# One-hot delivery of the last expert's rows to the first gate tile, and gate weights split earlier, in a hybrid transformer block

## The chip, the cores and the metric

The kernel runs on one core of one Trainium2 chip. The metric is the device time of one execution, in microseconds (us). Three runs of the kernel before took 1682.45, 1684.27 and 1686.49 us, with a median of 1684.27 us. The profile shown here is of one more execution, whose own time was 1682.92 us.

## The reference

One layer over 1024 tokens of width 1024, in float32:

```python
h = rms_norm(x, norm_mix);  z = h @ w_in
x = x + concat(pool_mix(z), neighbourhood_attention(z)) @ w_out
x = x + expert_choice_ffn(rms_norm(x, norm_ffn), w_router, w_gate, w_up, w_down)
g = sigmoid(rms_norm(x, norm_ple) @ w_ple_gate)
e = rms_norm(p @ w_ple_proj, norm_ple_post)
x = x + g * e
```

The expert part has 16 experts. Each picks its 128 best tokens (top-k over the tokens), so that a token can be picked by several experts or by none. For its tokens an expert computes `silu(xe @ w_gate) * (xe @ w_up) @ w_down` with 2048 hidden columns, scales the row by the token's affinity, and adds it to the token's row of the result. The change concerns the seam between this part and the last one, the gate: a product of all 1024 rows with a 1024 x 1024 matrix.

## The kernel before

**Staging.** The residual rows live in DRAM, as `acc_rows` (1024 x 1024). Each expert gathers its 128 rows by an indirect DMA on POOL's queue, computes, and adds its result `ye` to `acc_rows` by an indirect DMA with accumulation, also on POOL's queue (line 994: the scatter). After the last expert the gate reads `acc_rows` back in eight tiles of 128 tokens (`x2_0` to `x2_7`, line 1035; all of them are called x in the rows).

**Products.** Every float32 product is made of three passes over two-part numbers: an operand is split into `hi`, its rounded copy, and `lo`, what is left; `mm3` adds hi x hi (line 94), lo x hi (line 96) and hi x lo (line 98). A split takes one ACT instruction (line 85, or 88 with a gain) and one DVE instruction (line 86, or 89 with a gain). The left operand is split when its rows are transposed (`turn_rows`, line 931: four transposes of 128 x 128 on the tensor engine PE, then one split of 128 x 512).

**Weights.** Weights stream in as chunks of 256 x 1024 (1 MB) on the DMA queue of SP: 24 chunks for an expert and 4 for the gate, 388 in all, numbered through. `feed` splits half a chunk (128 x 1024) into a pair of buffers `fhi`, `flo`, of which there are four pairs (NH = 4). `product` uses the oldest split half and then calls `feed`, so that splitting runs four halves ahead of PE: each new ACT instruction waits until PE has left the buffer. Twelve raw slots go round in `ring`; when both halves of a chunk are split its slot is free and the next chunk is loaded into it, up to `NFREE = len(chunks) - 2`. With `feed(keep=True)` the split half goes to a raw slot instead of a buffer pair and stays there (called `fhl`).

**Order.** On PE, and in the expert stage on DVE and ACT too, instructions stand in the order of the program; after the expert stage (`steady.close()`) a scheduler sets the order on DVE and ACT. Each expert runs `expand` four times over (gate half 0, up half 0, gate half 1, up half 1: four steps of two products) and then `contract` (the down product into `pd`: eight steps kk of two products). During expert 14, `match` and `index` make expert 15's one-hot matrix `oh` of 128 x 1024, its token numbers `ix`, and start its gather.

**The seam.** During the last `contract`, the products' own `feed` calls split the last halves of the down weights and the first four halves of the gate weights. Then ACT scales `pd` into `ye` (line 993), the scatter is issued, and a gate chunk is loaded behind it on POOL's queue; SP loads `x2_0`, the last gate chunk, `x2_1` and `x2_2`. The rows of `x2_0` are transposed and split, the other four gate halves are split with `feed(True)`, and the eight embedding tiles `es` (128 x 1024 each) are multiplied by `g_post` on DVE (line 1082).

**The gate.** A gate block takes one tile of 128 tokens: 16 groups of three matmuls of 512 columns (two output halves j, eight steps k), with the transposes of the next tile put in front of groups 6 and 9. `sg` is the sigmoid of an output half (ACT, line 1062), multiplied by `es` and added to `x2` (DVE, lines 1063 and 1064) and stored.

## Time and profile before

| | us |
|---|---|
| median of three runs | 1684.27 |
| the profiled execution | 1682.92 |
| its span, first to last instruction | 1681.2 |
| PE busy | 1630.8 (97%) |
| DVE busy | 1347.5 (80%) |
| ACT busy | 1153.9 (69%) |
| POOL busy | 169.1 (10%) |

Section 2 of the page cuts the span into 40 slices; PE's busy share in tenths and the granted clock of PE read

```profile
PE   8999998998899999999999999999999999999698
PEclk9999999999999999999999999999999999999799
```

A slice is 42 us. PE is busy throughout the expert stage (slices 12 to 37), dips in slice 38, where the clock dips too, and is busy again to the end. Matmuls overlap their neighbours: a pass of 512 columns lasts 0.39 us in the rows, but the next one starts 0.227 us after it. So the start of an instruction is the better mark. "x2" behind a group means two instructions merged into a row, and the value in square brackets is the idle time of the engine ahead of them, with what ended it.

### The profile page before, as it was taken

The page shows a single profiled execution, that of the slowest core. Times are in us where ns is not written, and L with a number is a line of the kernel's source. Part 1 is how long each engine was busy: PE and PEld are TensorE (multiplying, and loading weights), DVE is VectorE, ACT ScalarE, POOL GpSimd, SP SyncE. Part 2 cuts the span into 40 slices and gives each one's busy share as a digit, 9 for nine tenths or more (in the row PEclk, how much of TensorE's full clock was granted, in tenths as well). Part 3 has the DMA queues.
Part 4 walks back from the last instruction along what each step waited for, and adds up shares of the span by engine and source line. Part 5 has one row for each costly group of instructions (what it writes and reads, how often), then busy time and mean ns, then how long its engine had stood idle before and what let it go on. Part 6 is the DMA issues. An engine that isn't in the chain of part 4 may idle for free.

```text
span 1681.2 us, 22945 instructions
## 1 busy us (share of the span) xinstructions
PE 1630.8 (97%) x8165; PEld 1368.0 (81%) x8165; DVE 1347.5 (80%) x1866; ACT 1153.9 (69%) x1471; POOL 169.1 (10%) x216
## 2 busy tenths in 40 slices
PE   8999998998899999999999999999999999999698
PEld 6889998886778888888888888888888888888587
DVE  4474555459879999999999999999999999999632
ACT  6254554432488888888888888888888888888431
POOL 1111112243310000000000000000000000000100
PEclk9999999999999999999999999999999999999799
DMA  6301201363699999999999999999999999996321
GB/s 187 116 29 33 66 26 51 92 204 97 216 365 373 401 371 400 377 368 408 373 391 385 367 403 377 378 399 369 399 378 367 410 370 392 386 368 242 106 98 59
DMA packets 129266, 470.54 MB, mean 280 GB/s; under 512 B 9600, under 2 KB 14720, under 8 KB 129152
## 3 DMA queue, kind: packets, MB, share of 16 engines
q1 hardware_dynamic: 122848, 445.80, 70.3%
q0 software_dynamic: 6304, 23.28, 5.3%
q8 instruction: 64, 1.05, 0.3%
q14 instruction: 50, 0.41, 0.1%
HBM read 448.00 MB, written 21.04 MB: 279 GB/s over the span
## 4 chain that ended last, share of the span: by engine, by line
PE 84%; DVE 7%; issue 4%; DMA 2%; POOL 1%; ACT 1%; SPq 0%; DVEq 0%; ACTq 0%; POOLq 0%
PE pu L94 7%; PE pu L96 7%; PE pu L98 7%; PE pg L94 6%; PE pg L96 6%; PE pd L96 6%; PE pd L94 6%; PE pg L98 6%; PE pd L98 6%; DVE both L581 3%; PE proj L94 2%; PE proj L98 2%; PE proj L96 2%; PE py L375 2%; PE pq L94 2%
## 5 line engine op out<-in xcount | busy, mean ns | idle before, releaser
L86 DVE TENSOR_TENSOR flo<-fraw,fhi 128x1024 fp32r<-128x1024 f32 x768 | 916.3, 1222 | 71.0 <-ACT fhi L85 33.5
L85 ACT ACTIVATE fhi<-fraw 128x1024 fp32r<-128x1024 f32 x768 | 809.4, 1061 | 192.6 <-PE pd L96 72.6
L94 PE MATMUL pd<-fhi,hidT 128*128 128x512 f32 x512 | 162.1, 398 | 0.0
L94 PE MATMUL pg<-fhi,xeT 128*128 128x512 f32 x512 | 159.2, 392 | 0.7 <-ACT xeT L85 0.7
L94 PE MATMUL pu<-fhi,xeT 128*128 128x512 f32 x512 | 159.2, 392 | 0.0
L96 PE MATMUL pd<-fhi,hidT 128*128 128x512 f32 x512 | 158.4, 390 | 0.0
L98 PE MATMUL pd<-flo,hidT 128*128 128x512 f32 x512 | 158.0, 390 | 0.0
L96 PE MATMUL pu<-fhi,xeT 128*128 128x512 f32 x512 | 158.0, 390 | 0.0
L96 PE MATMUL pg<-fhi,xeT 128*128 128x512 f32 x512 | 157.9, 389 | 0.0
L98 PE MATMUL pg<-flo,xeT 128*128 128x512 f32 x512 | 157.8, 389 | 0.0
L98 PE MATMUL pu<-flo,xeT 128*128 128x512 f32 x512 | 157.6, 389 | 0.0
L98 PEld LDWEIGHTS pd<-flo,hidT 128*128 128x128 f32 x512 | 96.1, 188 | 20.7
L96 PEld LDWEIGHTS pd<-fhi,hidT 128*128 128x128 f32 x512 | 96.1, 188 | 20.6
L96 PEld LDWEIGHTS pg<-fhi,xeT 128*128 128x128 f32 x512 | 96.0, 188 | 20.4 <-DVE xeT L86 0.4
L98 PEld LDWEIGHTS pu<-flo,xeT 128*128 128x128 f32 x512 | 96.1, 188 | 20.3
L96 PEld LDWEIGHTS pu<-fhi,xeT 128*128 128x128 f32 x512 | 96.1, 188 | 20.3
L98 PEld LDWEIGHTS pg<-flo,xeT 128*128 128x128 f32 x512 | 96.1, 188 | 20.1
L94 PEld LDWEIGHTS pg<-fhi,xeT 128*128 128x128 f32 x512 | 94.9, 188 | 19.7 <-ACT xeT L85 1.0
L94 PEld LDWEIGHTS pu<-fhi,xeT 128*128 128x128 f32 x512 | 95.0, 188 | 18.8
L94 PEld LDWEIGHTS pd<-fhi,hidT 128*128 128x128 f32 x512 | 92.8, 188 | 16.6
L994 POOL DMA_INDIRECT acc_rows<-ye,ix x16 | 26.6, 1661 | 764.0 <-ACT ye L993 764.0
L94 PE MATMUL proj<-wph,xT 128*128 128x384 f32 x256 | 99.8, 390 | 0.0
(215 smaller groups left out, 2341.0 us busy)
## 6 DMA issues: line engine op xcount, KB each, us to landing
fraw<-in_w_gate_dram SPq DMA_DIRECT2D x128, 1024.0 KB, 7.2
fraw<-in_w_down_dram SPq DMA_DIRECT2D x128, 1024.0 KB, 9.2
fraw<-in_w_up_dram SPq DMA_DIRECT2D x127, 1024.0 KB, 7.7
x<-in_x_dram SPq DMA_DIRECT2D x15, 512.0 KB, 4.9
wp_raw<-in_w_qkv_dram SPq DMA_DIRECT2D x16, 384.0 KB, 4.6
h_rows<-x POOLq DMA_DIRECT2D x8, 520.5 KB, 4.0
wo_raw<-in_w_out_dram SPq DMA_DIRECT2D x8, 512.0 KB, 3.4
acc_rows<-x SPq DMA_DIRECT2D x8, 512.0 KB, 4.6
```

The costliest lines, as they stand in the source:

```text
L85: ACT.activation(hi, src, AF.Copy)
L86: DVE.tensor_tensor(lo, src, hi.bitcast(F32), op=ALU.subtract)
L94: PE.matmul(outs[j], xh, wh[j], start=start, stop=False)
L96: PE.matmul(outs[j], xl, wh[j], start=False, stop=False)
L98: PE.matmul(outs[j], xh, wl[j], start=False, stop=stop)
L375: PE.matmul(pys[t][:, h], PTs[t, h][:, j * P:(j + 1) * P], vs[NU * pr + u0 + j][:, h * HD:(h + 1) * HD], start=(j == 0), stop=(j == u1 - u ...
L581: DVE.tensor_tensor(b[:, :, j], a[:, :, 0], a[:, :, 1], op=(ALU.max, ALU.min)[j])
L994: return POOL.indirect_dma_start(out=acc, out_offset=bass.IndirectOffsetOnAxis(ap=idxs[e][:, :1], axis=0), in_=ye, in_offset=None, compute ...
```

## The change

The rows of the last expert go two ways. They are still added to `acc_rows` by the scatter. In addition, `x2_0` is loaded during the last expert (behind step kk = 2 of its first up product), and the part of the last expert's result that belongs to tokens 0 to 127 is added to it on the core: `here` is a one-hot matrix (128 x 128, float32: row r has a one in the column of its token if that is below 128), and two float32 products `px = here^T ye` of 512 columns are added to `x2_0` by DVE. `ye` is made in two halves. Twelve transposes of the identity stand around the two products on PE.

The last `contract` splits more: `feed(True)` is called twice behind each of the steps 3, 4 and 5, the number of halves ahead grows to 6 and 8 and then falls to 0, so that the steps 6 and 7 feed nothing. All four gate chunks are loaded in the normal stream. The last two gate halves are split after the rows of `x2_0`. The `es` products may not be issued ahead of the split of those rows, and in gate block 0 the transposes of tile 1 stand in front of groups 13 and 15 in place of 6 and 9.

```diff
-    NFREE = len(chunks) - 2
+    NFREE = len(chunks)
...
+        if e == E - 1:
+            ixf = ixt[:, 1:2].bitcast(F32)
+            DVE.tensor_reduce(ixf, pi[:, 0:2], axis=AX.X, op=ALU.add)
+            here = fw.tile([P, D // 2], F32, tag="oh", name="here")
+            DVE.tensor_scalar(here[:, :P], iota, ixf, None, op0=ALU.is_equal)
+            ohs["first"] = here[:, :P]
...
     def product(po, xh, xl, start, stop):
         hi, lo = fed.pop(0)
         mm3([po[:, 0], po[:, 1]], xh, xl, halves(hi), halves(lo), start, stop)
-        if len(fed) < NH:
+        if len(fed) < ahead[0]:
             feed()
+
+    ahead = [NH]
...
-        ACT.activation(ye, pd.rearrange("p a b -> p (a b)"), AF.Copy, scale=xes[e][:, D + e:D + e + 1])
+        af = xes[e][:, D + e:D + e + 1]
+        if e < E - 1:
+            ACT.activation(ye, pd.rearrange("p a b -> p (a b)"), AF.Copy, scale=af)
+        else:
+            px = [fps.tile([P, 2, 512], F32, tag=t, name=f"px_{t}", bufs=1)[:, 0] for t in ("pg", "pu")]
+            wps = fps.tile([P, 4, P], F32, tag="tr", name="warm_ps3")
+            for i in range(8):
+                PE.transpose(wps[:, i % 4, :], ident, ident)
+            for h in range(2):
+                hs = slice(h * 512, (h + 1) * 512)
+                ACT.activation(ye[:, hs], pd[:, h], AF.Copy, scale=af)
+                PE.matmul(px[h], ohs["first"], ye[:, hs], start=True, stop=True)
+                DVE.tensor_tensor(x2s[0][:, hs], px[h], x2s[0][:, hs], op=ALU.add)
+            for i in range(4):
+                PE.transpose(wps[:, i, :], ident, ident)
         return POOL.indirect_dma_start(out=acc, out_offset=bass.IndirectOffsetOnAxis(ap=idxs[e][:, :1], axis=0),
                                 in_=ye, in_offset=None, compute_op=ALU.add)
...
+            if e == E - 1 and kk == 2:
+                load_x2(0)
...
+            if e == E - 1 and 3 <= kk < 6:
+                feed(True)
+                feed(True)
+                ahead[0] = (NH + 2, NH + 4, 0)[kk - 3]
...
-    with tc.issue_after(done.ins):
-        load_chunk(eng=POOL)
-    got = load_x2(0)
-    with tc.issue_after(got.ins):
-        load_chunk()
     for i in range(1, 3):
         load_x2(i)
     turn2(0, 0)
-    turn2(0, 1)
+    last = turn2(0, 1)
+    feed()
+    feed()
     norm2(0)
-    for _ in range(4):
-        feed(True)
-    for t in es:
-        for b in range(2):
-            DVE.tensor_tensor(t[:, b], t[:, b], gp, op=ALU.mult)
+    steady.close()
+    with tc.issue_after(last.ins):
+        for t in es:
+            for b in range(2):
+                DVE.tensor_tensor(t[:, b], t[:, b], gp, op=ALU.mult)
     for i in range(NU):
         sides = {}
         if i + 1 < NU:
-            sides[6] = [lambda i=i: turn2(i + 1, 0)]
-            sides[9] = [lambda i=i: turn2(i + 1, 1), lambda i=i: norm2(i + 1)]
+            sides[6 if i else 13] = [lambda i=i: turn2(i + 1, 0)]
+            sides[9 if i else 15] = [lambda i=i: turn2(i + 1, 1), lambda i=i: norm2(i + 1)]
```

On DVE, from the last down weights to the first output of the gate, the order before is this (fraw with its number is a raw chunk, hgT the split transposed rows of a gate tile):

```order
L89 SCALAR_TENSOR_TENSOR flo_0_14515<-fraw_14264,vec,fhi_0_14514 128x1024
L89 SCALAR_TENSOR_TENSOR flo_1_14525<-fraw_14264,vec,fhi_1_14524 128x1024
L1082 TENSOR_TENSOR es_4572<-es_4572,g_post 128x1024 x2
L1082 TENSOR_TENSOR es_4573<-es_4573,g_post 128x1024 x2
L1082 TENSOR_TENSOR es_4574<-es_4574,g_post 128x1024 x2
L1082 TENSOR_TENSOR es_4575<-es_4575,g_post 128x1024
L89 SCALAR_TENSOR_TENSOR fhl_0_14569<-fraw_14538,vec,fhl_0_14569 128x1024
L86 TENSOR_TENSOR hgT_14548<-tr_g_0_14549,hgT_14548 128x512
L86 TENSOR_TENSOR hgT_14548<-tr_g_1_14556,hgT_14548 128x512
```

and this in the changed kernel, from the last gate halves that are split ahead of `ye`:

```order
L88 SCALAR_TENSOR_TENSOR fhl_0_14509<-fraw_14294,vec,fhl_0_14509 128x1024
L88 SCALAR_TENSOR_TENSOR fhl_1_14512<-fraw_14294,vec,fhl_1_14512 128x1024
L1019 TENSOR_TENSOR x_0_14142<-px_pg,x_0_14142 128x512
L1019 TENSOR_TENSOR x_0_14142<-px_pu,x_0_14142 128x512
L86 TENSOR_TENSOR hgT_14572<-tr_g_0_14573,hgT_14572 128x512
L86 TENSOR_TENSOR hgT_14572<-tr_g_1_14580,hgT_14572 128x512
L1105 TENSOR_TENSOR es_4572<-es_4572,g_post 128x1024
L88 SCALAR_TENSOR_TENSOR flo_0_14588<-fraw_14316,vec,fhi_0_14587 128x1024
L88 SCALAR_TENSOR_TENSOR flo_1_14592<-fraw_14316,vec,fhi_1_14591 128x1024
```

The split of tile 0's rows has moved ahead of all `es` products, and two halves of gate weights stand behind the first of them. The next instructions of DVE there are

```order
L1105 TENSOR_TENSOR es_4572<-es_4572,g_post 128x1024
L1105 TENSOR_TENSOR es_4573<-es_4573,g_post 128x1024 x2
L1105 TENSOR_TENSOR es_4574<-es_4574,g_post 128x1024 x2
L1105 TENSOR_TENSOR es_4575<-es_4575,g_post 128x1024 x2
L1089 TENSOR_TENSOR sg_0_14636<-sg_0_14636,es_4572 128x512
L86 TENSOR_TENSOR hgT_14656<-tr_g_0_14657,hgT_14656 128x512
L1090 TENSOR_TENSOR sg_0_14636<-sg_0_14636,x_0_14142 128x512
L86 TENSOR_TENSOR hgT_14656<-tr_g_1_14670,hgT_14656 128x512
```

The split of tile 1's rows (hgT_14656) stands behind all eight `es` products and behind the first `sg` product; before, no `es` product stood between the two tiles' splits but one. On ACT, where the sums of squares (junkg) of tiles 1 and 2 stand ahead of the first sigmoid in both kernels, the changed order is

```order
L1017 ACTIVATE ye_14539<-pd_14359,xe_13553 128x512 x2
L1060 ACT_TABLE_LOAD
L1060 ACTIVATE warm_14562<-warm 128x1
L85 ACTIVATE hgT_14572<-tr_g_0_14573 128x512
L85 ACTIVATE hgT_14572<-tr_g_1_14580 128x512
L87 ACTIVATE fhi_0_14587<-fraw_14316,vec 128x1024
L87 ACTIVATE fhi_1_14591<-fraw_14316,vec 128x1024
L1066 ACTIVATE junkg_14596,ssqg_14595<-x_0_14142 128x1024
L1066 ACTIVATE junkg_14678,ssqg_14677<-x_1_14568 128x1024
L1066 ACTIVATE junkg_14743,ssqg_14742<-x_2_14570 128x1024
L1088 ACTIVATE sg_0_14636<-pq_0_14610,rstdg_14598 128x512
L85 ACTIVATE hgT_14656<-tr_g_0_14657 128x512
```

Here only two gate halves are left behind `ye`, against four before, and the split of tile 1's rows (last row) stands behind the first sigmoid, which stands behind the loads of tiles 1 and 2. On SP's queue the load of `x2_0` now stands in the weight stream, between the fifth and the sixth of the last eight down chunks; three down chunks, four gate chunks and `g_post` follow it, and then `x2_1` and `x2_2` with no weights between. On PE the products of the last `contract` stand as before; behind them stand the eight transposes, the two products with `here`, four transposes, and the transposes of tile 0, which wait for DVE's additions.

## Rows read from the trace of the kernel before

**Rows 1.** The chain that ended last, in order of time, from the last scatters to the first gate transposes: start (us), time (us), what.

```profile
1497.83 10.58 DMA acc_rows<-ye,ix
...
1565.00 7.38 DMA acc_rows<-ye,ix
1572.44 6.04 DMA x<-acc_rows
1578.61 1.94 PE tr_g L931 x8
```

**Rows 2.** The timeline of PE: the last pass of the last down product; the first group of gate block 0; the second pass of the first group of gate block 1.

```profile
1562.37 0.61 PE L98 MATMUL pd<-flo,hidT 128*128 128x512 f32 x2
...
1580.39 0.79 PE L94 MATMUL pq<-fhi,hgT 128*128 128x512 f32 x1
1581.11 0.79 PE L96 MATMUL pq<-fhi,hgT 128*128 128x512 f32 x1
...
1594.25 0.39 PE L96 MATMUL pq<-fhi,hgT 128*128 128x512 f32 x1
```

**Rows 3.** The timeline of DVE at the seam: splits of down halves (L86, 128x1024), of gate halves (L89), `es` products (L1082), and in gate block 0 the first `sg` instructions and the split behind them.

```profile
1543.34 4.62 DVE L86 TENSOR_TENSOR flo<-fraw,fhi 128x1024 fp32r<-128x1024 f32 x4
...
1549.08 10.38 DVE L86 TENSOR_TENSOR flo<-fraw,fhi 128x1024 fp32r<-128x1024 f32 x8
1559.68 5.35 DVE L89 SCALAR_TENSOR_TENSOR flo<-fraw,vec,fhi 128x1024 fp32r<-128x1024 f32 x4 [0.23 <-ACT fhi L88]
1564.96 8.03 DVE L1082 TENSOR_TENSOR es<-es,g_post 128x1024 f32<-128x1024 f32 x7
...
1582.96 3.67 DVE L89 SCALAR_TENSOR_TENSOR fhl<-fraw,vec,fhl 128x1024 fp32r<-128x1024 f32 x3
...
1589.80 0.69 DVE L1064 TENSOR_TENSOR sg<-sg,x 128x512 f32<-128x512 f32 x1
1590.41 0.69 DVE L86 TENSOR_TENSOR hgT<-tr_g,hgT 128x512 fp32r<-128x512 f32 x1
```

**Rows 4.** The timeline of ACT at the seam.

```profile
1545.35 1.07 ACT L85 ACTIVATE fhi<-fraw 128x1024 fp32r<-128x1024 f32 x1 [0.30 <-PE pd L96]
1546.31 1.07 ACT L85 ACTIVATE hidT<-tr_h 128x512 fp32r<-128x512 f32 x2
...
1551.69 1.06 ACT L85 ACTIVATE fhi<-fraw 128x1024 fp32r<-128x1024 f32 x1 [0.29 <-PE pd L96]
...
1562.57 1.15 ACT L88 ACTIVATE fhi<-fraw,vec 128x1024 fp32r<-128x1024 f32 x1 [0.21 <-PE pd L96]
1563.63 1.09 ACT L993 ACTIVATE ye<-pd,xe 128x1024 f32<-128x1024 f32 x1
...
1581.08 3.22 ACT L88 ACTIVATE fhl<-fraw,vec 128x1024 fp32r<-128x1024 f32 x3
```

**Rows 5.** Groups of instructions by line and shape on DVE and then on ACT, from 1400 us to the end: count, busy us, mean ns of one, idle before.

```profile
L89 DVE SCALAR_TENSOR_TENSOR fhl<-fraw,vec,fhl 128x1024 fp32r<-128x1024 f32 x4 | 5.0, 1279 | 5.4 <-ACT fhl L88 5.4
```

```profile
L1062 ACT ACTIVATE sg<-pq,rstdg 128x512 f32<-128x512 f32 x15 | 10.3, 690 | 37.0 <-PE pq L98 33.1 <-DVE hgT L86 3.9
L85 ACT ACTIVATE hgT<-tr_g 128x512 fp32r<-128x512 f32 x16 | 9.5, 595 | 24.8 <-PE tr_g L931 24.7
L1040 ACT ACTIVATE junkg<-x 128x1024 bf16<-128x1024 f32 x8 | 8.4, 1051 | 0.2
```

**Rows 6.** The timeline of PE where a plain float32 product of 128x512 runs (L286, one product, two instructions) with the next matmul behind it, and where eight transposes run at the full clock.

```profile
108.58 1.02 PE L286 MATMUL pool<-U,w_pool_sb 128*128 128x512 f32 x2
...
109.04 0.73 PE L94 MATMUL proj<-wph,xT 128*128 128x384 f32 x1
...
1409.12 1.03 PE L931 MATMUL tr_h<-ident,hid 128*128 128x128 f32 x8
```

**Rows 7.** DMA. First the issues of the last eight down chunks on SP's queue; then the median us from issue to landing of the down chunks from 1500 to 1540 us; then min, median and max of the eight loads of gate tiles (L1035).

```profile
1506.00 19.70 SPq L703 DMA_DIRECT2D fraw<-in_w_down_dram  x8
```

```profile
fraw<-in_w_down_dram SPq DMA_DIRECT2D x8, 1024.0 KB, 8.8
```

```profile
DMA to landing us min/median/max: 3.6/3.9/9.2
```

**Rows 8.** The clock. First stretches of 1 us: length, then busy time (and instructions) of PE, PEld, DVE, ACT and POOL, then the granted clock of PE, the DMA share and GB/s. Then the timeline of PE at the start of the program.

```profile
437.00:438.00 1.00, 1.00 (x3) 0.65 (x3) 0.90 (x6) 0.63 (x2) 0.23 (x1) 0.50 0.47 111
...
440.00:441.00 1.00, 1.00 (x10) 1.00 (x10) 0.96 (x4) 0.00 (x0) 0.00 (x0) 0.90 0.66 205
```

```profile
1566.00:1567.00 1.00, 0.00 (x0) 0.00 (x0) 1.00 (x2) 0.23 (x2) 1.00 (x1) 0.80 0.00 0
...
1583.00:1584.00 1.00, 1.00 (x5) 0.82 (x4) 1.00 (x2) 1.00 (x2) 0.00 (x0) 0.67 0.00 0
```

```profile
1.50 3.25 PE L217 MATMUL warm_ps<-ident 128*128 128x128 f32 x14 [1.50 <-POOL ident masks.py:199]
4.54 1.91 PE L185 MATMUL xt_ps<-ident,x 128*128 128x128 f32 x8
8.34 0.50 PE L94 MATMUL pu<-wuh,xT 128*128 128x512 f32 x1 [1.89 <-ACT wuh L88]
...
9.46 0.40 PE L94 MATMUL pu<-wuh,xT 128*128 128x512 f32 x1
...
10.20 0.63 PE L94 MATMUL pu<-wuh,xT 128*128 128x512 f32 x1
```

More of the change, by code (lines that the diff above doesn't have):

```diff
@@ L85, in split @@
             ACT.activation(hi, src, AF.Copy)
-            DVE.tensor_tensor(lo, src, hi.bitcast(F32), op=ALU.subtract)
-            return
+            return DVE.tensor_tensor(lo, src, hi.bitcast(F32), op=ALU.subtract)
         ACT.activation(hi, src, AF.Copy, scale=gain)
@@ L914, in index @@
             PE.matmul(pi[:, 0:2], oh[:, i], tokcol[:, i], start=(i == 0), stop=(i == NU - 1))
-        ix = fw.tile([P, 16], I32, tag="ix", name=f"ix_{e}", bufs=3)[:, 0:1]
+        ixt = fw.tile([P, 16], I32, tag="ix", name=f"ix_{e}", bufs=3)
+        ix = ixt[:, 0:1]
         with nc.allow_low_precision(reason="small integers"):
@@ L932, in turn_rows @@
         s = slice(4 * b, 4 * b + 4)
-        split(dst[:, 0, s], dst[:, 1, s], pt)
+        return split(dst[:, 0, s], dst[:, 1, s], pt)
     def halves(t):
@@ L940, in product, with load_x2 @@
         mm3([po[:, 0], po[:, 1]], xh, xl, halves(hi), halves(lo), start, stop)
-        if len(fed) < NH:
+        if len(fed) < ahead[0]:
             feed()
+    ahead = [NH]
+    x2s, hTs, r2 = {}, {}, {}
+    def load_x2(i):
+        x2s[i] = fw.tile([P, ROWP], F32, tag="xeT" if i % 3 == 2 else "xe", name=f"x2_{i}",
+                         bufs=1 if i % 3 == 2 else 2)
+        return SP.dma_start(x2s[i][:, :D], acc[i * P:(i + 1) * P, :])
     match(0)
@@ L1024, in block_kernel @@
                 bc_rows(gp, norm_ple_post[0], D)
-    steady.close()
     warm2 = tiny.tile([P, 1], F32, tag="warm2", name="warm2")
@@ L1029, in block_kernel @@
     fps = ctx.enter_context(pool("qps", 2, space=PSUM))
-    x2s, hTs, r2 = {}, {}, {}
-    def load_x2(i):
-        x2s[i] = fw.tile([P, ROWP], F32, tag="xeT" if i % 3 == 2 else "xe", name=f"x2_{i}",
-                         bufs=1 if i % 3 == 2 else 2)
-        return SP.dma_start(x2s[i][:, :D], acc[i * P:(i + 1) * P, :])
     def norm2(i):
@@ L1045, in turn2 @@
             hTs[i] = fw.tile([P, 2, KD, P], F32R, tag="hidT", name=f"hgT_{i}", bufs=2)
-        turn_rows(x2s[i], b, f"g{i}", hTs[i])
+        return turn_rows(x2s[i], b, f"g{i}", hTs[i])
     def gate_block(i):
```

## The prediction

> **What bounds the kernel now.** I read the page first: PE is busy 97% of the span, so only a stretch in which PE waits can be worth much. The chain of waits has one such stretch, the seam before the gate. The reader is to see there that nothing computes on the path: the scatter of the last expert is issued at 1565.00 and lands 7.38 us later, the reload of tile 0 takes 6.04 us more, and the transposes start at 1578.61 [rows 1]. PE's last down pass starts at 1562.37 and ends at 1562.98; the first gate pass starts at 1580.39 and the second at 1581.11 [rows 2]. Then the gate runs on PE without a gap to the end. So the mark that I follow is a pass late enough that both kernels are steady from there: the second pass of gate block 1, at 1594.25 [rows 2]. What the change moves this mark, it moves the end.
>
> Second, the rows of DVE and ACT at the seam [rows 3, 4]. They show what now lies in the gap for nothing: seven `es` products take DVE 8.03 us from 1564.96, while everyone waits for DMA. In the changed kernel there is no such gap, and this work comes onto DVE's way.
>
> **The change, part by part.** The wait for scatter and reload is removed for tile 0: its transposes wait for DVE's additions instead. I follow the new order engine by engine.
>
> *ACT.* The last half split at the old pace starts at 1551.69, when PE leaves its buffer [rows 4]. The ten that follow (four down, six gate halves) go to raw slots or to buffers that PE leaves in time, so ACT runs back to back: a down half starts 0.96 us after the one before (1545.35 to 1546.31), a gate half (3.22 - 1.15) / 2 = 1.04 us [rows 4]. Five steps of 0.96 and five of 1.04 put the last start at 1561.7 and its end at 1562.9. PE ends at 1562.98, so the first half of `ye` starts at about 1563.2. A half is 512 columns out of PSUM: 0.60 to 0.69 us by its neighbours [rows 5]. `ye` is complete at about 1564.5, against 1563.63 + 1.09 = 1564.72 [rows 4].
>
> *DVE.* It has the same ten halves, and is slower. Its first of them starts when the half from 1551.69 is through: that one ends on ACT at 1552.75 and starts on DVE at 1552.8. Back to back, a down half takes 4.62 / 4 = 1.16 us or a little less (the last row time includes the tail), a gate half (3.67 - 1.28) / 2 = 1.20 us [rows 3, 5]. So four down halves start from 1553.9, the first gate half at 1558.5, the sixth at 1564.5, and DVE is free at 1564.5 + 1.28 = 1565.8. Before, it was free at 1559.68 + 5.35 = 1565.03 with two halves less: there it waited for ACT (0.23 us idle in the row) [rows 3].
>
> *PE between.* A float32 product of 512 columns takes 1.02 us to its end, and the next matmul starts 0.46 us after it [rows 6]. The first product with `here` runs from about 1564.0, the second from 1564.7; both are done before DVE is free. They and the transposes around them cost nothing, since DVE covers them.
>
> *Tile 0.* DVE's two additions of 0.69 us start at 1565.8 and 1566.4 (0.61 us apart, as 1589.80 and 1590.41) [rows 3]. From the first transpose to the second gate pass there were 1581.11 - 1578.61 = 2.50 us at half clock [rows 1, 2]; eight transposes take 1.03 us at full clock against 1.94 [rows 6, 1], of which half lies on this path, so I take 2.2. The first addition ends at 1566.5, and the second pass of gate block 0 starts at 1568.7, against 1581.11: 12.4 us earlier.
>
> *Gate block 0.* Each group is three passes 0.227 us apart, 0.68 us. Thirteen groups and two sets of four transposes (0.45 us each) bring PE to block 1 at 1568.7 - 0.2 + 16 x 0.68 + 0.9 = 1580.3. But DVE has the longer list: the split of the second half of tile 0 to 1569.3, one `es` product (1.14), two gate halves (2.4), seven `es` products (8.03) [rows 3]: 1580.9. Behind them come the first `sg` product and then the split of tile 1, 0.61 us apart and 0.69 long: done at 1582.2. The second pass of block 1 waits for it. PE stands for about 1.7 us.
>
> *Tile 1's rows.* The scatter needs 7.38 us from its issue to landing, and the reload was issued 7.72 us after the end of `ye` (1564.72 to 1572.44) [rows 1, 4]. So tiles 1 and 2 are asked for at 1572.2. Reloads landed in 3.6 to 9.2 us, median 3.9 [rows 7]; the slow ones shared the DMA engines with two gate chunks, which are gone from there. Two tiles together take perhaps 5 us (my estimate, between the median and the 6.04 us of the first): 1577.3. ACT then squares tile 2 (about 1.3 us, by a 128x1024 instruction of 1.09 us) and makes the first sigmoid, at 1579.3. DVE is not ready for it until 1580.9. So this wait is covered, with 1.6 us to spare.
>
> *Loads and small things.* The load of `x2_0` is 0.5 MB in a stream that issues eight chunks of 1 MB in 19.70 us [rows 7]. With two gate chunks it adds 6 us of transfer. The last gate chunk follows the first of those eight by eleven places, so it is asked for at about 1537, and it is split after 1568: cover of some 30 us. Two small DVE instructions at expert 14 (128x1 and 128x128) lie beside PE's products. I cost both at nothing; without cover the load would cost its 1.3 us and the two instructions some tenths.
>
> The sum: 1594.25 - 1582.2 = 12.05 us, say 12.1. The profiled execution took 1682.92 us (its span 1681.2), so it would be 1670.8. The median of the runs is 1.35 us above that execution, so against the median: **1672.2 us**.
>
> The clock of PE is the term that rows do not settle. It fell after the last down product within about 4 us (1566 to 1567 shows 0.80, half from then on) and rose again around 1583, some 4 us after work began [rows 8]. In the changed kernel PE's idle pieces are all below 1 us, but most of the work in them is transposes. Here the rows say that transposes count: at the program's start 22 transposes ran at half-clock spacing (8 in 1.91 us), and the first matmuls behind them started 0.24 us apart, the full clock, before it fell at 10.20 [rows 8]. The Trainium skill, "TensorE: Matmul & The Clock Gate", Part 4: PE-mode transpose, says the opposite, that transpose-mode work does not count as PE being busy in the same way. By that rule the twelve identity transposes would not hold the clock, and the rival on the clock below would be the case; by the rows it is not. I go by the rows.
>
> **The rivals.**
>
> *The clock falls in the seam.* It was low for about 3 us at 437 to 440 [rows 8]. Three us of gate passes at half pace lose 1.5 us, the transposes of tile 0 0.4, the products with `here` nothing (DVE covers them). PE would reach block 1 at 1582.2, where DVE ends anyway; DVE's own start slips by 0.4. Saved 11.5 or so: 1672.8. For it: work in the seam is thin. Against it: the start of the program.
>
> *Tiles 1 and 2 come late.* The earlier scatter took 10.58 us under weight traffic [rows 1], and a reload has taken 9.2 [rows 7]. With 9.2 us from 1572.9 tile 2 lands at 1582.1; its squares, the sigmoid, the `sg` product and the split follow on (1.3 + 0.7 + 0.7 + 0.7): 1585.5. Saved 8.8: 1675.5. For it: the sigmoid stands behind both loads on ACT. Against it: the DMA engines are otherwise empty then.
>
> *DVE does not bind*, since the `es` products or the gate halves go faster than the rows: PE's own 1580.3 decides. Saved 13.9: 1670.4.
>
> *No gain*: tile 0's transposes turn out to wait for the scatter after all, or the loss of cover for 9.2 us of `es` products eats the rest. The order has no wait on the scatter there, so little speaks for it. 1681 to 1684.
>
> *Slower*: SP's queue is in order, and seven chunks now stand behind the load of `x2_0`, which must wait for the scatter of expert 14. That one landed at 1497.83 + 10.58 = 1508.4; the load's turn comes at about 1518 (five of eight chunks after 1506.00). So it passes at once. If something held it, the stock decides: the sixth down chunk, issued about 1518, is split at 1550.3, some 32 us later, and lands after 8.8 [rows 7], which leaves 23 us. Every us beyond is a us of PE. To lose the 12 us gained and 3.4 more it would have to be held for 38 us, to 1556, when the time would be 1687.7. I see nothing that would.
>
> **How the numbers follow.** Forecast 0.48 (1672.2, give or take 1); clock 0.14; late tiles 0.20; DVE not binding 0.10; no gain 0.05; slower 0.03. The run-to-run spread is about 2 us to each side of the median. The range reaches from 1669 (DVE not binding, less 1.4) to 1676.5 (late tiles, plus 1). A measurement of this kernel can tell 0.2%, 3.4 us, from no change. All cases but the last two save at least 8.8 us: faster 0.93. Of the no-gain case I put 0.04 within the bound, and slower is 0.03.
>
> **What the profile of the changed kernel would show.** Right: the first `hgT` split and gate pass at 1568 to 1569; DVE busy without a gap from 1552 to 1582 but for some 1 us at the transposes; the wait of PE ahead of block 1 put down to DVE's split of `hgT`, 1 to 2 us; the load of tile 2 landed by 1578.7; the granted clock at 1.0 from 1563 to 1585. Wrong: a gate pass spacing of 0.43 us in block 0; ACT's first sigmoid waiting for a load; PE waiting for a split inside the last `contract`; DMA waits of ACT after 1540.

## The result, and the profile after

The kernel before has a median of 1684.45 us (four runs, 1682.45 to 1686.49), the changed kernel of 1673.7 us (four runs, 1671.38 to 1677.14). The ratio is 0.9935 with a 95% interval of 0.9924 to 0.9947: 8.9 to 12.8 us less. Forecast were 1672.2 us and 12.1 us less. The profiled execution is the slowest of the four: 1677.14 us, span 1675.4.

All times below are from that execution; line numbers differ between the kernels (L93, L95 and L97 are the passes that were L94, L96 and L98). The two lines of the page that answer to those of the kernel before, PE's busy share and its granted clock in 40 slices:

```profile
PE   8999999998899999999999999999999999999998
PEclk9999999999999999999999999999999999999999
```

The dip of slice 38 is gone in both lines. The chain of waits through the seam (start, time, what), which answers to [rows 1]:

```profile
1569.30 2.47 DVE fhl L88 x2
1571.77 1.21 DVE x L1019 x2
1573.03 0.67 PE tr_g L937 x4
...
1577.88 1.28 DVE flo L88
1579.16 7.95 DVE es L1105 x7
1587.11 0.60 DVE sg L1089
1587.71 0.61 DVE hgT L86
```

No DMA is left in it: DVE carries it from the gate halves to the split of tile 1, but for the first transposes of tile 0 on PE and ACT's part of their split (1573.03 to 1574.35). PE's timeline, which answers to [rows 2] and, in its first row, to [rows 6]:

```profile
1415.17 1.04 PE L937 MATMUL tr_h<-ident,hid 128*128 128x128 f32 x8
...
1568.42 0.62 PE L97 MATMUL pd<-flo,hidT 128*128 128x512 f32 x2
...
1569.82 1.12 PE L1018 MATMUL px_pg<-ye,here 128*128 128x512 f32 x2
...
1573.03 1.09 PE L937 MATMUL tr_g<-ident,x 128*128 128x128 f32 x8 [0.79 <-DVE x L1019]
...
1575.10 0.50 PE L95 MATMUL pq<-fhl,hgT 128*128 128x512 f32 x1 [0.22 <-DVE hgT L86]
...
1588.37 0.50 PE L95 MATMUL pq<-fhl,hgT 128*128 128x512 f32 x1 [1.14 <-DVE hgT L86]
```

Absolute times mislead here: the last down pass starts at 1568.42, and in before at 1562.37 [rows 2]. So I measure in three pieces. From these transposes of the expert stage to the last down pass there are 1568.42 - 1415.17 = 153.25 us, in before 1562.37 - 1409.12 = 153.25 us [rows 2, 6]. From the last down pass to the second pass of gate block 1, called the **distance** from here on, there are 19.95 us, in before 31.88. From there to the end of the span there are 87.03 us, in before 86.95. So the change saves 11.93 us between the two marks. The first piece holds the last expert's one-hot products, the load of `x2_0`, the two further gate chunks and the early splits: together they cost PE nothing that the rows show. The 6.05 us by which all of it comes later were lost ahead of this piece, in code that the change leaves as it was: the scatter of the first expert is issued at 540.01 us in before and at 546.06 in the changed kernel, so the whole shift is there by then.

DVE, which answers to [rows 3]:

```profile
1569.30 2.47 DVE L88 SCALAR_TENSOR_TENSOR fhl<-fraw,vec,fhl 128x1024 fp32r<-128x1024 f32 x2
1571.69 0.68 DVE L1019 TENSOR_TENSOR x<-px_pg,x 128x512 f32<-128x512 f32 x1
1572.29 0.68 DVE L1019 TENSOR_TENSOR x<-px_pu,x 128x512 f32<-128x512 f32 x1
1574.35 1.29 DVE L86 TENSOR_TENSOR hgT<-tr_g,hgT 128x512 fp32r<-128x512 f32 x2 [1.38 <-ACT hgT L85]
1575.56 1.22 DVE L1105 TENSOR_TENSOR es<-es,g_post 128x1024 f32<-128x1024 f32 x1
1576.69 2.48 DVE L88 SCALAR_TENSOR_TENSOR flo<-fraw,vec,fhi 128x1024 fp32r<-128x1024 f32 x2
1579.08 8.03 DVE L1105 TENSOR_TENSOR es<-es,g_post 128x1024 f32<-128x1024 f32 x7
1587.03 0.69 DVE L1089 TENSOR_TENSOR sg<-sg,es 128x512 f32<-128x512 f32 x1
1587.63 0.68 DVE L86 TENSOR_TENSOR hgT<-tr_g,hgT 128x512 fp32r<-128x512 f32 x1
```

The `px` products of PE run while DVE is still at gate halves, so the additions wait for nothing. DVE has one gap, 1.38 us at the transposes of tile 0, and its last row releases PE. ACT, which answers to [rows 4], and the reload of tiles 1 and 2 on SP's queue, which answers to [rows 7]:

```profile
1569.08 1.26 ACT L1017 ACTIVATE ye<-pd,xe 128x512 f32<-128x512 f32 x2 [0.24 <-PE pd L97]
...
1581.50 1.06 ACT L1066 ACTIVATE junkg<-x 128x1024 bf16<-128x1024 f32 x1 [3.58 <-DMA x<-acc_rows]
...
1582.86 1.06 ACT L1066 ACTIVATE junkg<-x 128x1024 bf16<-128x1024 f32 x1 [0.20 <-DMA x<-acc_rows]
...
1583.91 0.67 ACT L1088 ACTIVATE sg<-pq,rstdg 128x512 f32<-128x512 f32 x1
```

```profile
1578.16 0.81 SPq L956 DMA_DIRECT2D x<-acc_rows  x2
```

The first sigmoid starts at 1583.91, and DVE takes it up only at 1587.03: the reload is covered. Two stretches of the granted clock, where 1.00 is the full clock and 0.50 half of it (length, busy time of PE, PEld, DVE, ACT, POOL, then the clock, the DMA share and GB/s), which answer to the 0.80 and 0.67 in [rows 8]; the other stretches of 1 us from 1555 to 1592 read 1.00 too:

```profile
1575.00:1576.00 1.00, 0.90 (x4) 0.77 (x5) 1.00 (x3) 1.00 (x2) 0.00 (x0) 1.00 0.91 160
...
1583.00:1584.00 1.00, 1.00 (x7) 0.79 (x6) 1.00 (x2) 1.00 (x3) 0.92 (x2) 1.00 0.00 0
```

### The profile page after: what moved, and what is told of

The parts are those of the page before. It is cut to its first block, busy times and chain, and to the rows that moved or that the text cites. A ratio compares the mean times of both kernels' runs of the same rounds, so it can differ in the third digit from the quotient of the medians.

```text
span 1675.4 us, 22979 instructions
## 1 busy us (share of the span) xinstructions
PE 1637.1 (98%) x8181; PEld 1372.4 (82%) x8181; DVE 1347.9 (80%) x1870; ACT 1152.5 (69%) x1472; POOL 171.7 (10%) x215
## 4 chain that ended last, share of the span: by engine, by line
PE 87%; DVE 7%; POOL 1%; ACT 1%; issue 1%; DMA 1%; SPq 0%; DVEq 0%; ACTq 0%; POOLq 0%
PE pu L93 8%; PE pu L95 8%; PE pu L97 8%; PE pg L93 7%; PE pg L95 7%; PE pg L97 7%; PE pd L95 7%; PE pd L93 7%; PE pd L97 7%; PE proj L93 2%; DVE both L580 2%; PE proj L97 2%; PE proj L95 2%; PE py L374 2%; PE tr_h L937 2%; PE pq L95 2%
## 5 line engine op out<-in xcount | busy, mean ns | idle before, releaser
L86 DVE TENSOR_TENSOR flo<-fraw,fhi 128x1024 fp32r<-128x1024 f32 x766 | 913.6, 1221 | 70.2 <-ACT fhi L85 33.5
L93 PE MATMUL pd<-fhi,hidT 128*128 128x512 f32 x508 | 160.9, 398 | 0.0
L93 PE MATMUL pg<-fhi,xeT 128*128 128x512 f32 x512 | 159.2, 392 | 0.8 <-ACT xeT L85 0.8
L93 PE MATMUL pu<-fhi,xeT 128*128 128x512 f32 x512 | 159.2, 392 | 0.0
L95 PE MATMUL pu<-fhi,xeT 128*128 128x512 f32 x512 | 158.0, 390 | 0.0
L95 PE MATMUL pg<-fhi,xeT 128*128 128x512 f32 x512 | 157.8, 389 | 0.0
L97 PE MATMUL pg<-flo,xeT 128*128 128x512 f32 x512 | 157.8, 389 | 0.0
L97 PE MATMUL pu<-flo,xeT 128*128 128x512 f32 x512 | 157.6, 389 | 0.0
L95 PE MATMUL pd<-fhi,hidT 128*128 128x512 f32 x508 | 157.1, 391 | 0.0
L97 PE MATMUL pd<-flo,hidT 128*128 128x512 f32 x508 | 156.8, 390 | 0.0
L97 PEld LDWEIGHTS pu<-flo,xeT 128*128 128x128 f32 x512 | 96.1, 188 | 20.4
L95 PEld LDWEIGHTS pg<-fhi,xeT 128*128 128x128 f32 x512 | 96.0, 188 | 20.4 <-DVE xeT L86 0.4
L95 PEld LDWEIGHTS pu<-fhi,xeT 128*128 128x128 f32 x512 | 96.1, 188 | 20.3
L97 PEld LDWEIGHTS pg<-flo,xeT 128*128 128x128 f32 x512 | 96.1, 188 | 20.1
L97 PEld LDWEIGHTS pd<-flo,hidT 128*128 128x128 f32 x508 | 95.3, 188 | 20.6
L95 PEld LDWEIGHTS pd<-fhi,hidT 128*128 128x128 f32 x508 | 95.3, 188 | 20.5
L93 PEld LDWEIGHTS pg<-fhi,xeT 128*128 128x128 f32 x512 | 94.8, 188 | 19.8 <-ACT xeT L85 1.1
L93 PEld LDWEIGHTS pu<-fhi,xeT 128*128 128x128 f32 x512 | 94.9, 188 | 18.8
L93 PEld LDWEIGHTS pd<-fhi,hidT 128*128 128x128 f32 x508 | 92.0, 188 | 16.4
L93 PE MATMUL proj<-wph,xT 128*128 128x384 f32 x256 | 100.3, 392 | 0.0
```

Source lines behind the costliest of these rows:

```text
L86: return DVE.tensor_tensor(lo, src, hi.bitcast(F32), op=ALU.subtract)
L93: PE.matmul(outs[j], xh, wh[j], start=start, stop=False)
L95: PE.matmul(outs[j], xl, wh[j], start=False, stop=False)
L97: PE.matmul(outs[j], xh, wl[j], start=False, stop=stop)
```

## The experiments

The theory was that of the prediction: one-hot delivery takes the scatter and the reload off tile 0's path, and then DVE's list sets the time. Each kernel is the changed one with an edit. What is compared is the distance, since single times differ by more than most edits are worth. Of the kernel before there is one trace, and so one distance. From the mark to the end of the span there are 86.8 to 87.0 us in every trace but one, which is named below.

**The changed kernel again.** No edit.

> The changed kernel as it is, once more, beside the two below. Theory: what the seam saves is fixed (distance from the last down pass to the second pass of gate block 1 again 19.9 to 20.0 us against 31.9), and the 6 us that the first profiled execution lost ahead of the expert stage are variation of unchanged code: the start of the last down pass in this run's trace lies anywhere from 1560 to 1570. Median 1671.5 to 1674.5. Rival: the change itself costs something ahead of the seam, and the last down pass starts at 1568 to 1569 again.

The median of six runs is 1674.02 us (1671.89 to 1674.84), beside 1684.52 us of before (eleven runs, 1680.28 to 1687.68): ratio 0.9938, interval 0.9923 to 0.9954. PE's timeline, with the same three marks:

```profile
1409.95 1.04 PE L937 MATMUL tr_h<-ident,hid 128*128 128x128 f32 x8
...
1563.20 0.62 PE L97 MATMUL pd<-flo,hidT 128*128 128x512 f32 x2
...
1583.15 0.50 PE L95 MATMUL pq<-fhl,hgT 128*128 128x512 f32 x1 [1.16 <-DVE hgT L86]
```

153.25 and 19.95 us again, and the end of the span (1670.1) lies 86.95 us behind. The last down pass starts 5.2 us earlier than in the first execution of the same kernel. So the shift is variation, and the rival falls. Both medians of the change save somewhat less (10.75 and 10.5 us) than the 11.93 us at the mark; their intervals cover the difference, and nothing here explains it further.

**Without the one-hot product.** Tile 0 waits for scatter and reload as before; the early splits of gate halves stay, and the `es` products stand in the gap.

```diff
-                PE.matmul(px[h], ohs["first"], ye[:, hs], start=True, stop=True)
-                DVE.tensor_tensor(x2s[0][:, hs], px[h], x2s[0][:, hs], op=ALU.add)
...
+    for i in range(3):
+        load_x2(i)
```

> The one-hot part is undone: tile 0 is loaded behind the scatter, as before, and ye is made in one piece. The early splits of gate weights, the early loads and the late transposes of tile 1 stay; the last two gate halves and the es products are put into the gap again. Read is the distance from the start of the last pass of the last down product to the start of the second pass of gate block 1: 31.9 us in the kernel before, 19.9 us in the changed one. Theory (the gain is the wait for scatter and reload of tile 0): the gap comes back. The reload is issued 9.7 us after the last pass, lands in about 3.5 us because no weights travel beside it, and the clock falls as before: 28.8 us. Rival (the gain is the early splitting and loading of the gate weights): about 20 us.

Measured: 30.81 us, 1683.44 us in one run (before beside it 1685.35). What is left of the change (early splits, early loads, the moved transposes of tile 1) saves 1.07 us of the 11.93. PE's wait and two stretches of the clock:

```profile
1577.34 1.94 PE L931 MATMUL tr_g<-ident,x 128*128 128x128 f32 x8 [12.69 <-DMA x<-acc_rows]
```

```profile
1569.00:1570.00 1.00, 0.00 (x0) 0.00 (x0) 1.00 (x2) 0.39 (x1) 0.00 (x0) 0.50 0.96 82
...
1584.00:1585.00 1.00, 1.00 (x3) 0.75 (x3) 0.00 (x0) 0.00 (x0) 0.22 (x1) 0.50 0.00 0
```

The number is 2 us over the expectation, and far from the rival's 20. From the first transpose to the second gate pass there are now 3.27 us, not 2.50, since PE waits 0.70 us for DVE's split; and PE ran at half clock until 1585, some 8 us after its work began again, where in before it rose after some 5. The expectation has no room for either.

**The one-hot product alone.** The early splits are undone: four gate halves are split behind tile 0.

```diff
-            if e == E - 1 and 3 <= kk < 6:
-                feed(True)
-                feed(True)
-                ahead[0] = (NH + 2, NH + 4, 0)[kk - 3]
...
-    feed()
-    feed()
+    for _ in range(4):
+        feed(True)
```

> The one-hot part alone: the last contract feeds as before (four gate halves), and the other four gate halves are split after the rows of tile 0, ahead of the es products. Same distance as in the first run (31.9 before, 19.9 changed). Theory (DVE's list sets the end of block 0): DVE has two gate halves fewer ahead of tile 0, but the additions wait for ye anyway, and two more behind it: 2 x 1.2 us, so 22 to 22.5 us, with PE waiting for gate halves 5 to 8 in block 0 and again for the split of tile 1. Rival (the early splits do nothing, the one-hot is all): 19.9 us.

Measured: 23.76 us (1680.76 us in one run): 8.1 us less than before, and 1.3 more than expected. PE waits 2.70 us for ACT ahead of block 1. ACT itself waited for POOL, which makes the reciprocal root that the first sigmoid needs. PE, ACT, POOL, and DVE beside it:

```profile
1589.58 0.50 PE L93 MATMUL pq<-fhi,hgT 128*128 128x512 f32 x1 [2.70 <-ACT hgT L85]
```

```profile
1588.35 0.69 ACT L1084 ACTIVATE sg<-pq,rstdg 128x512 f32<-128x512 f32 x1 [6.44 <-POOL rstdg L80]
```

```profile
1578.87 9.45 POOL L80 TENSOR_TENSOR rstdg<-rstdg,neghalf 128x1 f32<-128x1 f32 x1
```

```profile
1579.85 8.03 DVE L1101 TENSOR_TENSOR es<-es,g_post 128x1024 f32<-128x1024 f32 x7
```

An instruction on 128 numbers spans 9.45 us, and ends 0.4 us behind the `es` products. The distance does not show all that this wait costs: behind it the clock fell, from 1591 to 1594, and from the mark to the end there are 88.6 us, some 1.6 more than in the other traces.

```profile
1591.00:1592.00 1.00, 1.00 (x4) 0.81 (x3) 1.00 (x2) 0.00 (x0) 0.00 (x0) 0.53 0.16 59
```

The next experiment takes the root out of the way of the `es` products.

**The root early.** As the last one, with the sum of squares of tile 0 ahead of the gate halves.

```diff
-    for _ in range(4):
-        feed(True)
-    norm2(0)
+    norm2(0)
+    for _ in range(4):
+        feed(True)
```

> The kernel of e2, with the sum of squares of tile 0 (ACT) in front of the four gate halves, so that POOL makes its reciprocal root before the long run of es products on DVE and not beside it. Theory (in e2 POOL's power instruction of 0.55 us was held for 9.45 us by that run, and ACT's first sigmoid and the split of tile 1 behind it waited for that): POOL's two instructions take under 3 us together, PE's wait of 2.70 us for ACT ahead of block 1 goes, DVE's list alone decides, and the distance falls from 23.76 to 22.5 us (22.2 to 22.8). Rival (the wait in e2 comes from the late gate halves themselves): 23.4 to 24.5.

Measured: 22.48 us. PE's wait for ACT is gone, and it waits 0.89 us for DVE's split. POOL's rows of tile 0 and, behind them, the first of tile 1, which nobody needs yet:

```profile
1573.27 1.44 POOL L80 TENSOR_TENSOR rstdg<-rstdg,neghalf 128x1 f32<-128x1 f32 x1
1579.21 7.32 POOL L79 TENSOR_SCALAR rstdg<-ssqg 128x1 f32<-128x1 f32 x1 [4.49 <-ACT junkg L1062]
```

So the 1.3 us were the held root, and tile 1's was held in its turn. Taken in this order, one-hot delivery with all but the early splits makes 31.88 - 22.48 = 9.40 us of the whole gain, and the early splits on top of it 22.48 - 19.95 = 2.53 us. Without the one-hot product, the same splits and all the rest of the change are worth 1.07 us together, so the parts do not simply add.

**No identity transposes.** The twelve transposes around the `px` products are left out; they are no part of the result.

```diff
-            for i in range(8):
-                PE.transpose(wps[:, i % 4, :], ident, ident)
...
-            for i in range(4):
-                PE.transpose(wps[:, i, :], ident, ident)
```

> The twelve transposes of the identity around the two products with here are taken out; nothing else. They are no part of the result. Theory (the clock stays up without them, since PE's idle pieces in the seam stay below 1.5 us each): granted clock 1.0 throughout, distance 19.9 us within 0.3. Rival (the identity transposes hold the clock): the granted clock falls to 0.5 between 2 and 5 us after the last down pass, passes of block 0 start 0.43 us apart for about 3 us, distance 20 to 21.5 us.

Measured: 20.23 us (1676.84 us in one run). A stretch of its clock:

```profile
1576.00:1577.00 1.00, 1.00 (x4) 0.71 (x4) 1.00 (x2) 1.00 (x2) 0.00 (x0) 0.50 0.76 148
```

The clock fell to 0.50 from 1575 to 1578, in the middle of gate passes, some 7 us behind the last down pass. So the rival was right, though it had put the fall at 2 to 5 us. In the changed kernel the same passes run at 1.00, in both its traces; without the twelve transposes there is one trace. The fall cost only 0.28 us, because the slower PE spent the 1.14 us for which it would have waited for DVE.

**The gap filled with transposes.** The kernel without the one-hot product, with 100 transposes of the identity in PE's gap.

```diff
+            for i in range(100):
+                PE.transpose(wps[:, i % 4, :], ident, ident)
```

> The kernel of e1 (no one-hot), with 100 transposes of the identity on PE behind the last down product, about 11.7 us of them at 0.117 us each, which nearly fill the 12.7 us in which PE waited there at a falling clock. Theory (transposes hold the clock): 1.0 throughout; the first gate passes are still DVE's to release, so the second pass of block 0 stays near 16.6 and the 48 passes behind it run at full pace: 16.6 + 12.0 = 28.6 us to the mark (28.2 to 29.0). Rival, by the Trainium skill, TensorE: Matmul & The Clock Gate, Part 4: PE-mode transpose (transposes do not count as busy): the clock falls some 4 us behind the last product, the transposes left over run at half pace and overrun the reload, and the mark comes at 35 us or more; in no case below 30.8, what e1 measured.

Measured: 30.15 us (1683.5 us in one run, before beside it 1683.48). PE, and two stretches of the clock:

```profile
1565.25 11.08 PE L1006 MATMUL warm_ps<-ident 128*128 128x128 f32 x100
```

```profile
1575.00:1576.00 1.00, 1.00 (x12) 1.00 (x10) 1.00 (x2) 0.00 (x0) 0.00 (x0) 1.00 0.24 90
...
1583.00:1584.00 1.00, 1.00 (x4) 0.80 (x3) 0.00 (x0) 0.12 (x2) 0.72 (x2) 0.50 0.00 0
```

Through 11 us of nothing but transposes the clock stays at 1.00, where it fell within 4 us without them. The Trainium skill, "TensorE: Matmul & The Clock Gate", Part 4: PE-mode transpose, has it that transposes do not count as PE being busy in the same way; this run disagrees. My 28.6 us was missed all the same. Behind the transposes PE waited twice, 1.61 us for the reload and 1.59 us for DVE, and the clock then stood at 0.50 from 1583 to 1585. The 48 passes of block 0 took 13.6 us in place of the expected 12.0, which is the missing 1.5 us. The rival's 35 is far off, and 30.15 is under its floor of 30.8.

**Tile 1's transposes back at groups 6 and 9.**

```diff
-            sides[6 if i else 13] = [lambda i=i: turn2(i + 1, 0)]
-            sides[9 if i else 15] = [lambda i=i: turn2(i + 1, 1), lambda i=i: norm2(i + 1)]
+            sides[6] = [lambda i=i: turn2(i + 1, 0)]
+            sides[9] = [lambda i=i: turn2(i + 1, 1), lambda i=i: norm2(i + 1)]
```

> The change, but with the transposes of tile 1 in front of groups 6 and 9 of gate block 0, as before. Theory (the move to groups 13 and 15 is what covers the reload of tile 1): in the changed kernel group 6 starts at 1579.1 and tile 1's load ends at about 1581.4, so PE now waits 2.3 us there for the load. PE reaches the second pass of block 1 that much later, and DVE's split is ready by then: the distance from the last down pass to that pass is 19.95 - 1.14 + 2.3 = 21.1 us (20.8 to 21.5). Rival (DVE's list decides in any case): 19.4 to 20.0.

Measured: 22.88 us.

```profile
1576.90 0.63 PE L937 MATMUL tr_g<-ident,x 128*128 128x128 f32 x4 [2.47 <-DMA x<-acc_rows]
```

```profile
1579.00:1580.00 1.00, 1.00 (x3) 0.78 (x3) 1.00 (x2) 1.00 (x4) 0.98 (x1) 0.50 0.00 0
```

The wait is there, and the clock fell behind it (0.59, 0.50, 0.50, 0.70 from 1578 to 1582). Of the 1.8 us beyond the expectation the wait, longer than I had put it, makes 0.2, and the clock the other 1.6. So the two changed numbers in `sides` are worth 2.9 us: the wait of 2.47 and the 1.6 that the clock takes after it, less PE's old wait of 1.14.

**The `es` products late.** Only the first two stay ahead of tile 1's split; the others follow in the gate blocks.

```diff
-        for t in es:
-            for b in range(2):
-                DVE.tensor_tensor(t[:, b], t[:, b], gp, op=ALU.mult)
+        for b in range(2):
+            DVE.tensor_tensor(es[0][:, b], es[0][:, b], gp, op=ALU.mult)
...
+        if i < 3:
+            with tc.issue_after(turned[-1].ins):
+                for b in range(2):
+                    DVE.tensor_tensor(es[i + 1][:, b], es[i + 1][:, b], gp, op=ALU.mult)
```

> Six of the eight es products are made later, tile pair by tile pair, behind the split of the next tile's rows, from gate block 0 on. Theory (DVE's list, with eight es products ahead of the split of tile 1, holds up block 1): PE's wait of 1.1 us ahead of block 1 goes, distance 18.6 to 18.8 us. Rival (the load of tile 1 holds it up): distance 19.9 us as in the changed kernel, with PE or ACT waiting for the load.

Measured: 18.63 us, and PE no longer waits ahead of block 1:

```profile
1566.07 0.62 PE L97 MATMUL pd<-flo,hidT 128*128 128x512 f32 x2
...
1584.70 0.40 PE L95 MATMUL pq<-fhl,hgT 128*128 128x512 f32 x1
```

So DVE's list did bind, by the 1.3 us that went.

**The sum made in transposed form.** The `es` products stay late. For tile 0 PE adds the rows of `x2_0`, transposed, and `ye^T here` in PSUM, so that no DVE addition and no transpose stands behind `ye`; tile 0 is loaded once more for the residual.

```diff
+                PE.matmul(pts[k // 4][:, (k % 4) * P:(k % 4 + 1) * P], x2s[0][:, k * P:(k + 1) * P], ident,
+                          start=k % 4 == 0, stop=False)
...
+                    PE.matmul(pts[h][:, j * P:(j + 1) * P], ye[:, k * P:(k + 1) * P], ohs["first"],
+                              start=False, stop=j == 3)
```

> A version meant to be faster: the es products late as in e4; the transposed rows of tile 0 are made by accumulation in PSUM (rows of x2_0 times identity, plus ye chunk transposed times here), so DVE's two additions and the transposes behind them leave the path; tile 0 is loaded once more behind the scatter for the residual; one gate half less is split ahead of ye. Theory: ye's first half ends 1.3 us behind the last down pass's start, four products of 0.2 us and two splits of 0.6 us follow, second pass of block 0 at 3.6 to 4.2 us (6.68 in the changed kernel); then tile 1's reload, which ends at about 13, decides: mark at 16.0 to 16.9 us against 18.63 in e4. Rival (the reload of tile 1, now one of three, comes later, or the splits wait behind other work): 17.5 to 18.6.

Measured: 18.78 us, no better than the 18.63 with late `es` products, and even a little above the rival's range. The second pass of block 0 came at 6.38 us, hardly earlier than the 6.68 of the changed kernel.

```profile
1567.28 1.06 PE L1024 MATMUL pt_pg<-here,ye 128*128 128x128 f32 x8
...
1570.64 0.50 PE L93 MATMUL pq<-fhl,hgT 128*128 128x512 f32 x1 [1.41 <-DVE hgT L86]
```

Two mistakes of mine: the products with `ye` stood behind all those with `x2_0`, and the first gate pass waited until DVE had read the second half's sum, not only the first.

**The same, half by half.** Both mended, and timed beside the kernel with late `es` products.

```diff
+            pts = [fps.tile([P, 4, P], F32, tag="tr", name=f"pt_{h}") for h in range(2)]
...
+                for src, m in ((x2s[0], ident), (ye, ohs["first"])):
+                    for j in range(4):
```

> The kernel of e8 with its two faults mended: the products of the first half (x2_0, then ye) stand ahead of those of the second, no identity transposes, and the sums lie in the PSUM buffers of the transposes, so that the first gate pass need not wait until DVE has read the second half's sum. Theory: second pass of block 0 at 4.2 to 4.8 us behind the start of the last down pass (6.38 in e8, 6.68 in the changed kernel), mark at 16.6 to 17.4 us; time 2.5 to 3.3 us under the changed kernel's: 1668.8 to 1671.5. Rival (PE now reaches tile 1's transposes before its reload has landed, about 13 us behind the last down pass): mark at 17.4 to 18.6.

> The kernel of e4 (es products late), timed. Theory: 1.3 us less than the changed kernel timed beside it, as at the mark (18.6 against 19.95), 1670.3 to 1673.2; the intervals of the two will overlap. Rival: the same time as the changed kernel, or more, since the es products that now stand in later gate blocks hold DVE there.

Measured, half by half: the second pass of block 0 starts at 4.41 us, 2.3 us earlier than in the changed kernel, as expected; but the distance is 18.91 us, above both ranges. ACT shows why:

```profile
1581.97 1.06 ACT L1068 ACTIVATE junkg<-x 128x1024 bf16<-128x1024 f32 x1 [4.08 <-DMA x<-acc_rows]
...
1584.79 1.04 ACT L1068 ACTIVATE junkg<-x 128x1024 bf16<-128x1024 f32 x1
...
1585.82 1.07 ACT L85 ACTIVATE hgT<-tr_g 128x512 fp32r<-128x512 f32 x2
```

The split of tile 1 stands on ACT behind three sums of squares and a sigmoid, and the first of these waits for the second load of tile 0. PE also waits twice in block 0 for gate halves from DVE. It does not wait for the reload of tile 1, as the rival had it. What was gained ahead of block 0 was lost in it and ahead of block 1. The median is 1673.3 us (six runs, ratio 0.993, interval 0.9911 to 0.9949). With late `es` products the distance is 18.61 us and the median 1673.76 us (0.9938, 0.9922 to 0.9954). Both medians lie above what I had expected of them. Both kernels are faster than before; from the changed kernel, at 1674.02 us beside them, the runs cannot tell them, though the traces show 1.0 and 1.3 us less at the mark. So beyond late `es` products the transposed form gains nothing.

## Why the prediction was right

The sum: 12.05 us were forecast at the mark, 11.93 came. By the median of runs it was 10.75 us, and 10.5 beside the repeat; the intervals hold 11.9, and the spread of the unchanged part (5.2 us between two executions of the changed kernel) is larger than the difference. That the mark came within 0.12 us is in part luck: two errors, below, nearly cancel. I count from the start of the last down pass, at 1562.37 in the prediction and 1568.42 in the profile.

*`ye`* was forecast complete after 2.1 us and came after 1.92 (1570.34). *DVE free of its ten halves*: 3.4 forecast, 3.27 measured. The term holds.

*Tile 0*: second pass of block 0 forecast at 6.33, measured 6.68. The step that was off is the start of the transposes. I had them begin after the first addition; they began at 4.61, 0.06 us behind the second one, as the chain shows (both additions are one piece in it). Why they wait for both is not shown. From there to the second pass I took 2.2 us, where the terms beside it give 2.50 less half of 0.91, or 2.05; 2.07 came. The late start went into DVE's list too: the split of tile 0 ended at 7.22 for 6.93. The rest of that list took 0.2 us less than I had put, which made up for it.

*The race to block 1*: forecast were DVE's end at 19.83 and PE, without the wait, at 18.16 (1580.3 and one pass of 0.23). Measured were 19.89 (the pass follows at 19.95) and 18.81 (1588.37 less 1.14). DVE's list was right to 0.06 us. PE came 0.65 later, so it waited 1.14 instead of 1.7 us: 0.35 of that is tile 0's late start, and the rest block 0, which took 12.13 us from second pass to second pass, not 11.83. ("Thirteen groups" there should read sixteen, which is what the sum uses.) That DVE binds is shown by the late `es` products: they took that wait away and moved the mark by 1.32 us.

*Tiles 1 and 2*: asked for at 9.74 us (9.83 forecast), tile 2's squares begin at 14.44 (14.9 forecast for its landing), the first sigmoid is done at 16.16 (16.9). DVE takes it at 18.61, so 2.4 us are to spare, not 1.6. The rival of late tiles did not come about, nor that of no gain: tile 0's transposes wait 0.79 us for DVE's addition, and nothing on PE's path waits for the scatter. What I had not named is how much of this cover lies in the move of the transposes to groups 13 and 15: without it PE waits 2.47 us. One sign of being wrong that I had named is there all the same, a DMA wait of ACT after 1540: ACT waits 3.58 us for tile 1's load. The sign was too wide, since this wait is covered.

*Loads and small things*, costed at nothing: the 153.25 us ahead of the last down pass are equal to 0.01 us. The slower case, SP's queue held behind `x2_0`, leaves no trace in the rows.

*The clock* stayed at 1.0 as forecast. I had given two reasons at once, that PE's pauses are all below 1 us and that transposes count. The first was wrong by my own sum, which has PE stand 1.7 us ahead of block 1 (1.14 came). The second is what the runs bear out: 100 transposes alone held the clock, and without the twelve (pauses of 0.78 and 1.24 us in their place) it fell for some 3 us, the rival that I had priced at 0.6 us more. It cost 0.28. Short pauses with nothing in them were not tried by themselves.

## What to carry to other kernels

When a round trip through DRAM bounds a seam, deliver the first tile on the core and let the round trip run behind it; then list what each engine did in the gap for nothing, since that list is the next bound, and move the consumers of the rows still in flight as late as their own cover allows. Judge such an edit by the distance between two marks of one trace: it repeated to 0.02 us here, where whole runs differ by 5 us. Look at the stretch behind the second mark too, since a wait just ahead of it can take the clock down behind it (1.6 us in one run here). Filling a short pause of PE with transposes kept its clock here, and a wait of 2.5 us on PE cost 1.6 more through the clock.

## What the runs showed of the hardware

Transposes of the identity held the granted clock at 1.00 for 11 us, and when PE waited 1.6 us twice soon after them it fell to 0.50. Behind waits of 2.47 and 2.70 us it fell to 0.50 for some 3 us; behind one of 1.14 us it stayed at 1.00.

A POOL instruction of 0.55 us on 128 numbers spanned 9.45 us beside a run of seven DVE products of two SBUF operands, and another 7.32 us beside six; in the kernel with the root early, moving it in time ended PE's wait. (Spans on POOL are rough, but ACT's wait for it ended where the 9.45 us do, at 1588.35.) The Trainium skill, "SBUF — State Buffer", Who interferes with whom, says that a DVE instruction with two SBUF inputs contends with a GpSimd instruction that reads SBUF; these rows agree. In the changed kernel the same POOL instruction beside the same seven products took 1.44 us, in both its profiles. What makes the difference was not tried and stays open.
